# A hybrid encoder layer on one core: low parts of the mix weights moved to VectorE, the first norm's setup reordered, and the last down products written out in order

## The chip, the cores and the metric

The kernel runs on one core of a Trainium2 chip. The metric is the device time of one execution in microseconds (us). The core has TensorE for matrix products, VectorE, ScalarE and GpSimd for the rest, and a sequencer, SyncE (SP), which here only issues DMAs. The profile calls them PE (PEld for its weight loads), DVE, ACT, POOL and SP. TensorE's results go to PSUM, eight banks of 128 x 512 f32.

## The reference

One encoder layer over 512 tokens of width 1024, all in float32:

```
h = layer_norm(x, ln_in_g, ln_in_b)
mix = parallel_mixer(h, ...)      # window attention and dilated attention, each rms-normed,
                                  # side by side, times w_mix_out (1024 x 1024)
h = layer_norm(ALPHA * h + mix, ln1)
h = layer_norm(ALPHA * h + memory_cross_attention(h, mem_n), ln2)
ff = (gelu(conv3(h @ w_gate)) * (h @ w_up)) @ w_down     # inner width 2816
out = layer_norm(ALPHA * h + ff, ln3)
```

## The kernel before, in words

**Products.** Each float32 operand of a large product is split into a high part `hi` (a copy in a shorter format, ScalarE, line 136) and a low part `lo = raw - hi` (line 138), and a product is three matmuls: hi by hi, hi by lo, lo by hi (`mm`, line 168). Weights arrive in tiles `raw` of 128 x 1024 f32 (512 KB; three buffers) and become `hi` and `lo` (six buffers each). The low part is made on VectorE unless a caller names another engine; before the change `load_win` and `load_dil` name `nc.gpsimd` for the eight tiles of `w_mix_out`.

**Tokens** stand in four blocks `b` of 128. Accumulators are PSUM tiles: tags `t` and `o` with one bank each, `g` with two tiles of one bank, `s` with two tiles of two banks. A tile of two banks is one tile to the program that places waits: whoever writes one of its halves waits for those who read the other.

**Order.** Where the code stands in `manual_schedule(engines=...)`, the named engines run in the order of the text. Elsewhere a planner orders each engine's instructions by its own estimate of when they can run; `pin()` holds the next product at its place in the text. In the start (from line 371) TensorE, VectorE and ScalarE keep the order of the text; in the mix and behind it only TensorE does. The gate, up and down loops, from line 1350 on, are planned.

**Start.** `x` and the first weights of `w_in` are loaded on SP's queue. The first norm's scale and shift (`ln_in_g`, `ln_in_b`) are brought to all partitions by a product: `rows` (the tile `vt`) is zeroed, 128 x 1024 for each, one row of it is filled by a DMA, and a tile of ones (in `zs`) times it fills PSUM. The scale goes from there to `gin` by ScalarE (line 382), the shift stays in PSUM (an `s` tile, both halves). A float32 matmul of this kind is two instructions. `busy(n)` issues n products of the ones tile with itself, as work that nobody reads: `WARM[0]` of them ahead of the scale's product, `WARM[1]` behind the shift's. Then for block 0: `gain` (line 338: less the mean, times the scale), `shift` (line 345: times the root, plus the shift) on VectorE, and `turn` (line 352), transposes with `ident`, a part of the constants `cst`.

**Mix.** After attention the dilated outputs `oA` and `oB` are combined column tile by column tile (lines 1043 to 1051, `split_gain` at 924 and 925), while TensorE works at the memory's keys and values and then at the mix: for each half of the columns `load_win`, and for each block four k tiles of products into a `g` tile, which line 1119 adds to `h` on VectorE. Only then is the `g` tile free for the block after next. `load_dil` and the dilated part follow.

**Down.** 22 k tiles of `w_down`; the accumulators of all four blocks stand in PSUM together: block 0 in `t` and `o`, blocks 1 and 3 in one `s` tile each, block 2 in two `g` tiles. The first 16 k tiles go k by k over all blocks. For the last six the text goes block by block, half by half of the columns, and behind each half VectorE adds it to `h` (line 1408) and takes its statistics (1411). Behind both come `moments`, the norm (1415, 1416), and the output's DMA on SP (1417). Which block's products come when is the planner's.

Of the kernel before, what the change touches and what calls it, by code (L numbers as in the profile page):

```python
# [9 lines left out]
F32 = mybir.dt.float32  # L10
# [38 lines left out]
]  # L49

MEM_AT = (2, 0)
WARM = (6, 6)
CI, CF, CS, CMA, CM1, CM3 = 0, 128, 129, 130, 514, 770
CW = 898

# [16 lines left out]
def hymba_layer(ctx: ExitStack, tc: tile.TileContext, A, cst_d, out):  # L72
# [16 lines left out]
    cst = cpool.tile([P, CW], F32, name="cst")  # L89
    ident = cst[:, CI : CI + P]  # L90
    mhalf = cpool.tile([P, 1], F32, name="mhalf")
    nc.vector.memset(mhalf, -0.5)
    ones = cpool.tile([P, 2], F32, name="ones")
    nc.vector.memset(ones, 1.0)
    halfpi = cpool.tile([P, 1], F32, name="halfpi")
    nc.vector.memset(halfpi, HALF_PI)
    def halves(t):
        return [t[:, i * 512 : (i + 1) * 512] for i in range(2)]

# [41 lines left out]
    def wsplit(raw, shape, eng=None):  # L141
        return split(raw, shape, wpool, "hi", 6, wpool, "lo", 6, eng)
# [52 lines left out]
    def ps_tile(tag, bufs, shape=None):  # L195
        return gpool.tile(shape or [P, 512], F32, tag=tag, bufs=bufs, name=tag)
# [44 lines left out]

    zs = mkv.tile([P, 4, S], F32, tag="km", name="zs")
    ones_t = zs[:, 0, 0:P]
    nc.vector.memset(ones_t, 1.0)
    vt = mkv.tile([P, NB, 512], F32, tag="vm", name="vt")
    rows = vt.rearrange("p (v n) f -> p v n f", v=2)
    for v, name in enumerate(("ln_in_g", "ln_in_b")):
        nc.vector.memset(rows[:, v], 0.0)
        nc.scalar.dma_start(rows[0:1, v].rearrange("p n f -> p (n f)"), A[name].partition_broadcast(1))
    nc.scalar.dma_start(cst[:, 0:CMA], cst_d[:, 0:CMA])  # L250
    gin = wpool.tile([P, D], F32, tag="gb", bufs=2, name="gin")
    gt = halves(gin)
    sbt = s_tile()
# [115 lines left out]
        nc.scalar.dma_start(h_dram[b * P : (b + 1) * P, :], ah)  # L369

    with tc.manual_schedule(engines={nc.tensor.engine, nc.vector.engine, nc.scalar.engine}):
        spare = ps_tile("t", 1)

        def busy(n, ps=None):
# [556 lines left out]
    with tc.manual_schedule(engines={nc.tensor.engine}):  # L931
# [160 lines left out]
        def load_win(c0):  # L1092
            wa = w_mix[0:512, c0 : c0 + 512].rearrange("(s j d) f -> s d j f", s=2, d=HD)
            wts = []
            for i in range(2):
                raw = wpool.tile([P, 2, 512], F32, tag="raw", bufs=3, name="raw")
                for s2 in range(2):
                    nc.sync.dma_start(raw[s2 * HD : (s2 + 1) * HD], wa[s2][:, 2 * i : 2 * i + 2, :])
                wts.append(wsplit(raw, [P, 2, 512], nc.gpsimd))
            return wts  # L1100

        def load_dil(c0):
            return [w_rows(w_mix, 4 + 2 * i, 2, c0, 512, nc.gpsimd) for i in range(2)]

        def mix_part(ps, wts, b, k0, t):
            for k in range(4):
# [261 lines left out]
    with gs:  # L1368
        acc = [[ps_tile("t", 1), ps_tile("o", 1)]]
        for b in range(1, NB):  # L1370
            two = s_tile() if b != 2 else None
            acc.append([g_tile(), g_tile()] if two is None else [two[:, i, :] for i in range(2)])
        KO = NF - 6

        def down_q(k, w, a, b, f, a_):
            whi, wlo = w
            ahi, alo = a
            t = slice(b * P, (b + 1) * P)
            o = acc[b][f.start // 512][:, a_]
            mm(o, ahi[:, t], whi[:, 0, f], k == 0, False)  # L1380
            mm(o, ahi[:, t], wlo[:, 0, f], False, False)
            mm(o, alo[:, t], whi[:, 0, f], False, k == NF - 1)

        def down_k(k, w, a, b):
            for i in range(2):
                down_q(k, w, a, b, slice(i * 512, (i + 1) * 512), slice(0, 512))

        def down_ops(k):
            w = w_rows(A["w_down"][0], k, 1, 0, D)
            a = split(act[:, k, :], [P, S], xpool, "x", 12, xpool, "x", 12)  # L1390
            return w, a

        for k in range(KO):
            w, a = down_ops(k)
            for b in range(NB):
                down_k(k, w, a, b)
        last = [down_ops(k) for k in range(KO, NF)]
        o2 = out.rearrange("o s d -> (o s) d")
        for b in range(NB):
            q = 2  # L1400
            st = spool.tile([P, q, 6], F32, tag="stq", bufs=1, name="st")
            w_ = D // q
            for i in range(q):
                f = slice(i * w_, (i + 1) * w_)
                a_ = slice(i * w_ % 512, i * w_ % 512 + w_)
                for n, (w, a) in enumerate(last):
                    down_q(KO + n, w, a, b, f, a_)
                nc.vector.scalar_tensor_tensor(  # L1408
                    h[b][:, f], h[b][:, f], ALPHA, acc[b][i * w_ // 512][:, a_], ALU.mult, ALU.add
                )  # L1410
                nc.vector.bn_stats(st[:, i, :], h[b][:, f])
            mv, rs = moments(st)
            for i in range(2):
                f = slice(i * 512, (i + 1) * 512)
                nc.vector.scalar_tensor_tensor(h[b][:, f], h[b][:, f], mv[:, 0:1], g3[:, f], ALU.subtract, ALU.mult)
                nc.vector.scalar_tensor_tensor(h[b][:, f], h[b][:, f], rs, b3[:, f], ALU.mult, ALU.add)
                nc.sync.dma_start(o2[b * P : (b + 1) * P, f], h[b][:, f])


_INS = [  # L1420
# [25 lines left out]
```

## Time and profile before

| | us |
|---|---|
| three runs | 930.78, 929.01, 922.87 |
| their median | 929.01 |
| the profiled execution | 924.79 |
| its span, first to last instruction | 922.9 |
| mean granted TensorE clock | 0.995 |

The profile is of one execution. Rows of the time line give start, duration, engine, line, operation, out<-in, shapes and count of merged instructions; brackets give the idle time of the engine ahead of it and what ended it. A matmul is shown longer than its place in the pipeline: 128x512 is shown as 0.39 us, while the starts stand 0.227 us apart. Engine names ending in q are DMA issues.

### The profile page before, as it was taken

The numbers are of one execution on the slowest core, as the hardware profiler recorded it, in microseconds if no ns is written. First come the engines' busy times: TensorE is split into PE (matmuls) and PEld (weight loads), VectorE is DVE, ScalarE is ACT, GpSimd is POOL, SyncE is SP. The second block draws the span as 40 slices with busy tenths as digits, with TensorE's granted clock in tenths as the row PEclk, the third lists the DMA queues.
The fourth block names the chain that finished last, engine by engine and source line by source line (L and its number), as shares of the span: only waits on it lengthen the run. The fifth ranks groups of instructions, "written<-read, shape, count | busy, mean of one in ns | idle before, by whom it ended". The sixth has DMA issues, their size and how long they took to land.

```text
span 922.9 us, 12172 instructions
## 1 busy us (share of the span) xinstructions
PE 904.8 (98%) x4803; PEld 759.9 (82%) x4803; DVE 499.0 (54%) x853; ACT 361.9 (39%) x636; POOL 147.4 (16%) x109
## 2 busy tenths in 40 slices
PE   8999999999999999899999999999999999999996
PEld 6778987898878898688988889888888888888885
DVE  7965145435456666769466585554334434433346
ACT  4573436416455576215454223442233233222310
POOL 0054024332444426310000010000000000000001
PEclk9999999999999999999999999999999999999998
DMA  5762041314222337315222315433333332223201
GB/s 215 215 219 69 23 137 47 90 48 116 69 69 69 92 124 207 125 47 162 90 69 69 92 31 157 117 109 94 108 94 92 93 112 92 92 92 101 81 24 69
DMA packets 116939, 92.80 MB, mean 101 GB/s; under 512 B 12472, under 2 KB 100752, under 8 KB 116882
## 3 DMA queue, kind: packets, MB, share of 16 engines
q1 hardware_dynamic: 116048, 89.80, 32.1%
q10 hardware_dynamic: 834, 2.22, 0.6%
q8 instruction: 38, 0.62, 0.3%
q14 instruction: 19, 0.16, 0.1%
HBM read 87.82 MB, written 4.19 MB: 100 GB/s over the span
## 4 chain that ended last, share of the span: by engine, by line
PE 54%; DVE 2%; DMA 0%; issue 0%; ACT 0%; DVEq 0%; ACTq 0%
PE g L168 25%; PE s L168 21%; PE t L168 4%; PE o L168 4%; PE s L208 1%; DMA raw<-in_w_up_dram 0%; PE s L1220 0%; DVE lo L138 0%; DVE sd L1051 0%; DVE Ulo L214 0%; DVE mx L1201 0%; DVE h L126 0%; DVE h L124 0%; DVE h L1408 0%; ACT hi L136 0%
## 5 line engine op out<-in xcount | busy, mean ns | idle before, releaser
L138 DVE TENSOR_TENSOR lo<-raw,hi 128x1024 fp32r<-128x1024 f32 x134 | 167.2, 1248 | 153.5 <-ACT hi L136 151.2
L136 ACT CAST hi<-raw 128x1024 fp32r<-128x1024 f32 x142 | 149.2, 1052 | 225.4 <-PE g L168 151.0
L109 POOL TENSOR_TENSOR rs<-ve,mhalf 128x1 f32<-128x1 f32 x18 | 15.3, 852 | 534.6 <-DVE ve L115 526.3
L168 PE MATMUL g<-Thi,hi 128*128 128x512 f32 x240 | 94.9, 395 | 0.0
L168 PE MATMUL g<-Tlo,hi 128*128 128x512 f32 x240 | 94.4, 393 | 0.0
L168 PE MATMUL g<-Thi,lo 128*128 128x512 f32 x240 | 94.1, 392 | 0.0
L168 PE MATMUL g<-Uhi,hi 128*128 128x512 f32 (+1 forms) x256 | 93.3, 364 | 0.0
L168 PE MATMUL g<-Uhi,lo 128*128 128x512 f32 (+1 forms) x256 | 92.9, 363 | 0.0
L168 PE MATMUL g<-Ulo,hi 128*128 128x512 f32 (+1 forms) x256 | 92.9, 363 | 0.0
L525 POOL TENSOR_TENSOR zs<-zs,rsn 128x512 f32<-128x512 f32 x29 | 59.3, 2045 | 147.3 <-DVE zs L524 147.3
L168 PE MATMUL g<-hi,Thi 128*128 128x512 f32 x184 | 72.4, 403 | 3.5 <-DVE h L1119 3.5
L168 PE MATMUL g<-hi,Tlo 128*128 128x512 f32 x184 | 71.8, 400 | 0.5 <-DVE Tlo L1168 0.5
L168 PE MATMUL g<-lo,Thi 128*128 128x512 f32 x184 | 71.2, 398 | 0.4 <-DVE lo L279 0.4
L168 PE MATMUL s<-Uhi,lo 128*128 128x512 f32 x160 | 62.3, 390 | 0.0
L168 PE MATMUL s<-Ulo,hi 128*128 128x512 f32 x160 | 62.3, 390 | 0.0
L168 PE MATMUL s<-Uhi,hi 128*128 128x512 f32 x160 | 62.3, 389 | 0.0
L523 DVE TENSOR_TENSOR zs<-g,rc 128x512 f32<-128x512 f32 x29 | 20.0, 688 | 68.4 <-PE g L168 31.5
L168 PEld LDWEIGHTS g<-Uhi,lo 128*128 128x128 f32 x256 | 48.3, 189 | 7.5
L168 PEld LDWEIGHTS g<-Ulo,hi 128*128 128x128 f32 x256 | 48.3, 189 | 7.4
L168 PEld LDWEIGHTS g<-Uhi,hi 128*128 128x128 f32 x256 | 48.3, 189 | 7.4
L168 PEld LDWEIGHTS g<-Thi,hi 128*128 128x128 f32 x240 | 45.1, 188 | 11.0 <-issue 0.9
L168 PEld LDWEIGHTS g<-Tlo,hi 128*128 128x128 f32 x240 | 45.1, 188 | 10.3 <-issue 1.4
(330 smaller groups left out, 1796.5 us busy)
## 6 DMA issues: line engine op xcount, KB each, us to landing
raw<-in_w_in_dram SPq DMA_DIRECT2D x37, 512.0 KB, 3.8
raw<-in_w_gate_dram SPq DMA_DIRECT2D x22, 512.0 KB, 3.8
raw<-in_w_up_dram SPq DMA_DIRECT2D x22, 512.0 KB, 3.9
raw<-in_w_down_dram SPq DMA_DIRECT2D x22, 512.0 KB, 3.2
raw<-in_w_xk_dram SPq DMA_DIRECT2D x8, 512.0 KB, 3.9
raw<-in_w_xv_dram SPq DMA_DIRECT2D x8, 512.0 KB, 3.3
raw<-in_w_xq_dram SPq DMA_DIRECT2D x8, 512.0 KB, 4.7
raw<-in_w_xo_dram SPq DMA_DIRECT2D x8, 512.0 KB, 3.3
```

The lines of the kernel that those rows point to most:

```text
L109: nc.gpsimd.tensor_tensor(out_, in_, mhalf, ALU.pow)
L136: nc.scalar.copy(hi, raw)
L138: (eng or nc.vector).tensor_tensor(lo, raw, hi.bitcast(F32), ALU.subtract)
L168: on_pe(nc.tensor.matmul(o, l, r, start=first, stop=last))
L208: on_pe(nc.tensor.transpose(ps[:, i // 4, f : f + P], t[:, i * P : (i + 1) * P], ident))
L523: nc.vector.tensor_tensor(zc, ps, rc, ALU.mult)
L525: nc.gpsimd.tensor_tensor(sh, sh, rsn, ALU.mult)
```

## The change

`WARM` goes from (6, 6) to (12, 3). The ones tile, the zeros of the shift row and the three small constants go from VectorE to GpSimd; the zeros of the scale row stay on VectorE, which has no memset ahead of them any more. The three DMAs of ScalarE's queue (scale row, shift row, constants) go into the block in which ScalarE keeps the order of the text; before, they stood ahead of it and the constants were issued first. The low parts of the mix weights go from GpSimd to VectorE. The last six k tiles of the down products go into a block in which TensorE keeps the order of the text: blocks 1, 3, 0, 2, both halves of a block's products ahead of the additions and statistics of either.

```diff
--- before.py
+++ after.py
@@ -49,7 +49,7 @@
 ]
 
 MEM_AT = (2, 0)
-WARM = (6, 6)
+WARM = (12, 3)
 CI, CF, CS, CMA, CM1, CM3 = 0, 128, 129, 130, 514, 770
 CW = 898
 
@@ -89,11 +89,9 @@
     cst = cpool.tile([P, CW], F32, name="cst")
     ident = cst[:, CI : CI + P]
     mhalf = cpool.tile([P, 1], F32, name="mhalf")
-    nc.vector.memset(mhalf, -0.5)
     ones = cpool.tile([P, 2], F32, name="ones")
-    nc.vector.memset(ones, 1.0)
     halfpi = cpool.tile([P, 1], F32, name="halfpi")
-    nc.vector.memset(halfpi, HALF_PI)
+
     def halves(t):
         return [t[:, i * 512 : (i + 1) * 512] for i in range(2)]
 
@@ -241,13 +239,13 @@
 
     zs = mkv.tile([P, 4, S], F32, tag="km", name="zs")
     ones_t = zs[:, 0, 0:P]
-    nc.vector.memset(ones_t, 1.0)
+    nc.gpsimd.memset(ones_t, 1.0)
     vt = mkv.tile([P, NB, 512], F32, tag="vm", name="vt")
     rows = vt.rearrange("p (v n) f -> p v n f", v=2)
-    for v, name in enumerate(("ln_in_g", "ln_in_b")):
-        nc.vector.memset(rows[:, v], 0.0)
-        nc.scalar.dma_start(rows[0:1, v].rearrange("p n f -> p (n f)"), A[name].partition_broadcast(1))
-    nc.scalar.dma_start(cst[:, 0:CMA], cst_d[:, 0:CMA])
+    for v in range(2):
+        (nc.vector, nc.gpsimd)[v].memset(rows[:, v], 0.0)
+    for t, value in ((mhalf, -0.5), (ones, 1.0), (halfpi, HALF_PI)):
+        nc.gpsimd.memset(t, value)
     gin = wpool.tile([P, D], F32, tag="gb", bufs=2, name="gin")
     gt = halves(gin)
     sbt = s_tile()
@@ -369,6 +367,9 @@
         nc.scalar.dma_start(h_dram[b * P : (b + 1) * P, :], ah)
 
     with tc.manual_schedule(engines={nc.tensor.engine, nc.vector.engine, nc.scalar.engine}):
+        for v, name in enumerate(("ln_in_g", "ln_in_b")):
+            nc.scalar.dma_start(rows[0:1, v].rearrange("p n f -> p (n f)"), A[name].partition_broadcast(1))
+        nc.scalar.dma_start(cst[:, 0:CMA], cst_d[:, 0:CMA])
         spare = ps_tile("t", 1)
 
         def busy(n, ps=None):
@@ -1096,11 +1097,11 @@
                 raw = wpool.tile([P, 2, 512], F32, tag="raw", bufs=3, name="raw")
                 for s2 in range(2):
                     nc.sync.dma_start(raw[s2 * HD : (s2 + 1) * HD], wa[s2][:, 2 * i : 2 * i + 2, :])
-                wts.append(wsplit(raw, [P, 2, 512], nc.gpsimd))
+                wts.append(wsplit(raw, [P, 2, 512]))
             return wts
 
         def load_dil(c0):
-            return [w_rows(w_mix, 4 + 2 * i, 2, c0, 512, nc.gpsimd) for i in range(2)]
+            return [w_rows(w_mix, 4 + 2 * i, 2, c0, 512) for i in range(2)]
 
         def mix_part(ps, wts, b, k0, t):
             for k in range(4):
@@ -1396,25 +1397,22 @@
                 down_k(k, w, a, b)
         last = [down_ops(k) for k in range(KO, NF)]
         o2 = out.rearrange("o s d -> (o s) d")
-        for b in range(NB):
-            q = 2
-            st = spool.tile([P, q, 6], F32, tag="stq", bufs=1, name="st")
-            w_ = D // q
-            for i in range(q):
-                f = slice(i * w_, (i + 1) * w_)
-                a_ = slice(i * w_ % 512, i * w_ % 512 + w_)
-                for n, (w, a) in enumerate(last):
-                    down_q(KO + n, w, a, b, f, a_)
-                nc.vector.scalar_tensor_tensor(
-                    h[b][:, f], h[b][:, f], ALPHA, acc[b][i * w_ // 512][:, a_], ALU.mult, ALU.add
-                )
-                nc.vector.bn_stats(st[:, i, :], h[b][:, f])
-            mv, rs = moments(st)
-            for i in range(2):
-                f = slice(i * 512, (i + 1) * 512)
-                nc.vector.scalar_tensor_tensor(h[b][:, f], h[b][:, f], mv[:, 0:1], g3[:, f], ALU.subtract, ALU.mult)
-                nc.vector.scalar_tensor_tensor(h[b][:, f], h[b][:, f], rs, b3[:, f], ALU.mult, ALU.add)
-                nc.sync.dma_start(o2[b * P : (b + 1) * P, f], h[b][:, f])
+        pin()
+        with tc.manual_schedule(engines={nc.tensor.engine}):
+            for b in (1, 3, 0, 2):
+                st = spool.tile([P, 2, 6], F32, tag="stq", bufs=1, name="st")
+                fs = [slice(i * 512, (i + 1) * 512) for i in range(2)]
+                for f in fs:
+                    for n, (w, a) in enumerate(last):
+                        down_q(KO + n, w, a, b, f, slice(0, 512))
+                for i, f in enumerate(fs):
+                    nc.vector.scalar_tensor_tensor(h[b][:, f], h[b][:, f], ALPHA, acc[b][i], ALU.mult, ALU.add)
+                    nc.vector.bn_stats(st[:, i, :], h[b][:, f])
+                mv, rs = moments(st)
+                for f in fs:
+                    nc.vector.scalar_tensor_tensor(h[b][:, f], h[b][:, f], mv[:, 0:1], g3[:, f], ALU.subtract, ALU.mult)
+                    nc.vector.scalar_tensor_tensor(h[b][:, f], h[b][:, f], rs, b3[:, f], ALU.mult, ALU.add)
+                    nc.sync.dma_start(o2[b * P : (b + 1) * P, f], h[b][:, f])
 
 
 _INS = [
```

## Rows read from the trace of the kernel before

**Rows 1.** The page, busy time of the engines: us, share of the span, instructions.

```profile
PE 904.8 (98%) x4803; PEld 759.9 (82%) x4803; DVE 499.0 (54%) x853; ACT 361.9 (39%) x636; POOL 147.4 (16%) x109
```

**Rows 2.** The view by stretches: the stretch and its length, then busy us (instructions) of PE, PEld, DVE, ACT and POOL, the granted clock, the DMA engines' share, GB/s.

```profile
0.00:13.00 13.00, 9.29 (x32) 6.16 (x32) 6.41 (x14) 3.40 (x4) 0.75 (x5) 1.00 0.87 329
13.00:41.00 28.00, 27.07 (x137) 21.96 (x137) 26.34 (x45) 17.36 (x25) 1.63 (x3) 1.00 0.54 157
...
402.00:432.00 30.00, 30.00 (x146) 25.11 (x147) 27.75 (x45) 9.52 (x12) 3.98 (x4) 1.00 0.30 87
...
910.00:923.00 13.00, 4.59 (x19) 3.30 (x18) 8.60 (x16) 0.00 (x0) 1.83 (x2) 0.79 0.30 110
```

**Rows 3.** The time line of the first 14 us, all engines.

```profile
0.73 0.41 ACTq L250 DMA_DIRECT2D cst<-in_constants_dram  x1
...
0.80 0.06 DVE L92 MEMSET mhalf<- 128x1 f32 x1 [0.80 <-PEq L1431]
...
1.14 2.93 PE L168 MATMUL t<-zs 128*128 128x128 f32 x12 [1.14 <-DVE zs L244]
...
1.25 0.91 DVE L248 MEMSET vt<- 128x1024 f32 x1 [0.16 <-issue]
...
2.19 0.49 ACTq L249 DMA_DIRECT2D vt<-in_ln_in_g_dram  x1
...
6.64 3.38 PE L168 MATMUL g<-vt,zs 128*128 128x512 f32 x4 [2.58 <-DMA vt<-in_ln_in_g_dram]
...
9.86 1.88 PE L168 MATMUL s<-vt,zs 128*128 128x512 f32 x4
...
11.58 1.50 PE L168 MATMUL t<-zs 128*128 128x128 f32 x12
...
11.84 1.41 DVE L345 SCALAR_TENSOR_TENSOR oA<-oA,rs,s 128x512 f32<-128x512 f32 x2 [0.41 <-PE s L168]
...
13.14 0.65 PE L352 MATMUL t<-cst,oA 128*128 128x128 f32 x4
```

**Rows 4.** The time line of GpSimd near 343 us: a memset of 512 columns.

```profile
343.33 0.52 POOL L1001 MEMSET stw<- 128x512 f32 x1
```

**Rows 5.** Groups of instructions by form, 340 to 405 us: the low parts on GpSimd and on VectorE. Busy us, mean ns of one, idle time ahead of them.

```profile
L138 POOL TENSOR_TENSOR lo<-raw,hi 128x1024 fp32r<-128x1024 f32 x8 | 21.2, 2666 | 18.0 <-ACT hi L136 17.9
...
L138 DVE TENSOR_TENSOR lo<-raw,hi 128x1024 fp32r<-128x1024 f32 x5 | 6.1, 1220 | 4.1 <-ACT hi L136 4.1
```

**Rows 6.** The time line in the mix: GpSimd, then VectorE.

```profile
356.20 16.06 POOL L138 TENSOR_TENSOR lo<-raw,hi 128x1024 fp32r<-128x1024 f32 x6 [5.88 <-ACT hi L136]
...
361.54 0.69 DVE L1043 TENSOR_TENSOR oA<-oA,s 128x512 f32<-128x512 f32 x1 [1.86 <-PE s L168]
...
362.86 1.97 DVE L1045 TENSOR_TENSOR oA<-oA,oB 128x512 f32<-128x512 f32 x1
...
367.04 2.98 DVE L925 SCALAR_TENSOR_TENSOR Tlo<-oA,gdc,Thi 128x512 fp32r<-128x512 f32 x1 [1.02 <-ACT Thi L924]
369.94 2.87 DVE L1045 TENSOR_TENSOR oA<-oA,oB 128x512 f32<-128x512 f32 x1
373.60 0.75 DVE L925 SCALAR_TENSOR_TENSOR Tlo<-oA,gdc,Thi 128x512 fp32r<-128x512 f32 x1 [0.79 <-ACT Thi L924]
...
375.47 0.74 DVE L1119 SCALAR_TENSOR_TENSOR h<-g,raw__3058,h 128x512 f32<-128x512 f32 x1
...
377.33 0.69 DVE L1045 TENSOR_TENSOR oA<-oA,oB 128x512 f32<-128x512 f32 x1
...
379.79 0.74 DVE L925 SCALAR_TENSOR_TENSOR Tlo<-oA,gdc,Thi 128x512 fp32r<-128x512 f32 x1
...
387.20 2.88 DVE L1051 TENSOR_TENSOR sd<-sd,oB 128x512 f32<-128x512 f32 x1
390.00 1.40 DVE L1119 SCALAR_TENSOR_TENSOR h<-g,raw__3058,h 128x512 f32<-128x512 f32 x2
```

**Rows 7.** The time line of TensorE about its two waits in the mix.

```profile
373.28 0.39 PE L168 MATMUL g<-hi,Tlo 128*128 128x512 f32 x1
376.27 0.50 PE L168 MATMUL g<-hi,Thi 128*128 128x512 f32 x1 [2.60 <-DVE h L1119]
...
389.52 0.39 PE L168 MATMUL g<-hi,Tlo 128*128 128x512 f32 x1
390.80 0.50 PE L168 MATMUL g<-hi,Thi 128*128 128x512 f32 x1 [0.89 <-DVE h L1119]
```

**Rows 8.** The view by stretches, columns as in rows 2: the stretch from 378.4 us.

```profile
378.40:381.50 3.10, 3.10 (x8) 2.45 (x8) 2.73 (x5) 0.89 (x2) 0.00 (x0) 0.50 0.45 169
```

**Rows 9.** The last down products: a row of the chain of waits (start, us, what) where they begin; the time line of VectorE at the last k tile and at the end, and of TensorE at the end.

```profile
881.66 3.40 PE t L168 x15
...
883.08 1.23 DVE L138 TENSOR_TENSOR lo<-raw,hi 128x1024 fp32r<-128x1024 f32 x1 [0.26 <-ACT hi L136]
...
915.41 0.69 DVE L1408 SCALAR_TENSOR_TENSOR h<-h,s 128x512 f32<-128x512 f32 x1 [0.91 <-PE s L168]
...
909.83 0.39 PE L168 MATMUL s<-hi,lo 128*128 128x512 f32 x1
911.00 0.50 PE L168 MATMUL s<-hi 128*128 128x512 f32 x1 [0.78 <-DVE h L1408]
...
914.99 0.39 PE L168 MATMUL s<-hi,lo 128*128 128x512 f32 x1
```

## The prediction

> **What bounds the kernel now.** First the page's table of engines: TensorE is busy for 904.8 of the 922.9 us span, VectorE for 499.0 [rows 1]. So an edit pays only where it removes idle or slow TensorE time, 18 us of idle in all. The view by stretches says where that lies [rows 2]: 3.71 us in the first 13 us (9.29 busy), 0.93 us from 13 to 41 and none from 402 to 432, although VectorE works 26.34 of 28 and 27.75 of 30 us there, and 8.41 us in the last 13 us. The time line then names the wait at each place: the first norm's scale row [rows 3], `h`, line 1119, twice in the mix [rows 7], and `h`, line 1408, once in the last down products [rows 9]. The three edits of the change lie at these three places, so their savings add. Between them TensorE's order is written out or pinned and it works without rest, so an earlier arrival at 13 us, at 402 us and at 881 us is kept.
>
> **Start.** Now VectorE makes three small memsets and the ones tile, and zeroes the scale row from 1.25 to 2.16. The row's DMA is issued at 2.19, the product that waits for it starts at 6.64, 4.45 us later, after TensorE has rested for 2.58 us [rows 3]. With the row's memset first on VectorE (from 0.80, the start of its first one) and 0.91 us long, the issue comes at 1.74, 0.45 us sooner. With the same 4.45 us the products can start at 6.19.
>
> Whether the 24 warm-up instructions (two for each of 12 calls) are done by then, and at which clock the rest runs, decides the size. The granted clock reads 1.00 from 0 to 13 us [rows 2], but the durations show two levels a factor of two apart, 1.2 and 2.4 GHz: twelve warm-up instructions take 2.93 us at the start and 1.50 us from 11.58; the four of the scale row take 3.22 us from start to start (6.64 to 9.86), the four of the shift row 1.72 (9.86 to 11.58) [rows 3]. Before the pace rose, TensorE had worked from 6.64 on; in the first stretch, 1.14 to 4.07, it rested before it could rise. The change replaces this rest by work. All 24 at the low level take 24 x 0.244 = 5.9 us and end at 7.0; with seven or more of them at the high one they end by 6.2. I take the high level from 6.2 on: scale row 6.2 to 7.9, shift row to 9.64, against 11.58: 1.94 us sooner. Of the closing warm-up 6 instructions go instead of 12 (0.75 us), to about 10.4, so it is not late. VectorE's shift waits for both halves of the shift row, now 0.26 us (11.84 against 11.58), then works 1.41 us: its end moves from 13.25 to 11.31, and with it the transposes of 13.14. **Start: 1.9 us.** Bounds: all warm-up and scale products at the low level, 7.0 + 3.22 + 1.72 = 11.94, a loss of 0.4; a row that lands 0.5 us sooner still, because the constants' DMA no longer stands ahead of it on ScalarE's queue, a gain of 2.4.
>
> What is moved costs nothing by these covers. The ones tile, the shift row's zeros and three small constants go to GpSimd: 512 columns take 0.52 us there [rows 4], so 1024 take about 1.0 and the shift row's DMA can go at about 2.3, right behind the scale row's, where it went at 3.27; its product is wanted at 7.9. TensorE's first product waits for the ones tile on GpSimd, now the first thing there. The constants' DMA, 65 KB, drops from 0.73 to about 2.5, third on ScalarE's queue ahead of its first copy, and is wanted by the transposes at 11; with DMA engines full from 3 to 14 us it may take 6 us and still land by 9. No queue of SP is changed.
>
> No row shows a memset of VectorE beside one of GpSimd. The nearest are two-input operations of both, where VectorE's takes up to 2.2 us more [rows 6]. If the memset suffered the whole length of GpSimd's, 1.0 us, the issue would be at 2.7 and the start's gain some 1.0 us. I keep 1.74, since neither memset reads anything. The Trainium skill ("SBUF — State Buffer", Who interferes with whom) says that a VectorE instruction with at most one SBUF input, outside its two-port modes, doesn't contend with GpSimd; by it the sum stays at 1.9, by the stretched rows it would be 1.0. No run here shows it yet.
>
> **Mix weights.** GpSimd makes eight low parts at 2.666 us each; VectorE makes the same tile in 1.220 [rows 5]. So VectorE gets 8 x 1.22 = 9.8 us more. But while GpSimd works, VectorE's own operations stretch: `oA`, line 1045, takes 1.97 and 2.87 us against 0.69, `Tlo`, line 925, 2.98 against 0.74, and `sd`, line 1051, of the same shape as `oA`, 2.88 [rows 6]. That is 1.28 + 2.24 + 2.18 + 2.19 = 7.9 us on these four alone, and all four stand ahead of an addition (line 1119) that TensorE waits for.
>
> First stall: from 361.54 to 375.47 VectorE's row of operations leads to the addition of block 0, which gives back the accumulator that TensorE wants at 373.5 (0.23 after its product of 373.28); it gets it at 376.27 [rows 6, 7]. Lost: 2.99 - 0.23 = 2.76 us. Behind the stall the granted clock falls to 0.50, the 1.2 GHz level, for 378.4 to 381.5 [rows 8]: half of 3.1 us, 1.55 us, is lost too. After the change this stretch loses 5.7 us of stretching and gains about three of the low parts, 3.7 us (GpSimd begins six at 356.20, so the first three have their place before 361.5). The addition then starts 2.0 us sooner, at 373.5, and TensorE goes on 0.8 us later as now, at 374.3: 0.8 us of stall are left if nothing else moves. Of the present 13.9 us VectorE also spends 1.8 waiting, 1.02 of it ahead of 367.04 for ScalarE's `Thi`, which itself follows a stretched line 1045; without that no stall is left. A stall of 0.8 us ended at full clock at 390.80 [rows 7], so I count the slow stretch as gone either way. Second stall: 389.52 to 390.80, less 0.23, 1.05 us, where `sd` at 2.88 stands ahead of the addition of 390.00 [rows 6, 7]. After it two low parts on VectorE (2.4 us) replace the stretch, but VectorE has been free for some 3 us before, since the first stall is gone. Sum 2.76 + 1.55 + 1.05 = 5.4; with a rest of 0.4 us, **5.0 us**. Bounds: 5.4, and for the other end the third rival. What is next late is VectorE itself in 402 to 432, 27.75 busy of 30 [rows 2], which the change leaves alone. GpSimd has nothing else to do here.
>
> **Last down products.** 144 products lie in 881.7 to 915.4. They follow each other 0.227 us apart but for one place: block 3's second half stands in the shared two-bank tile whose first half VectorE must first read (line 1408); 909.83 to 911.00 [rows 9], 0.94 us too long, and a first step of about 0.1 more. In the written order both halves of a block are multiplied before either is read, and the blocks in shared tiles (1, 3) come first. So the wait has no place, and block 2, last, has a tile for each half: its first half is read during the second, as now. The tail from the last product, 914.99, to VectorE's read at 915.41 and the span's end stays as it is. Price of the order: six rows of k stand in the first half of block 1, the last one wanted 15 products after 881.66, at 885.06. Its low part begins at 883.08, behind the high one, and is done at 884.31 [rows 9]; 0.75 us of room. If planning delays them by 1 us, 0.25 us is lost. **1.0 us**, bounds 0 and 1.05.
>
> **Sum.** 1.9 + 5.0 + 1.0 = 7.9 us. The profiled execution took 924.79 us, 922.9 of span and 1.9 around it; by it the new time is 916.9. The three shown runs are 922.87 to 930.78 with the median at 929.01, so the profiled one is a low draw. The middle of the four times, 926.9, less 7.9 gives **919.0**.
>
> **Rivals.** (1) The mix pays nothing: the low parts stand ahead of the additions on VectorE's queue, waiting for ScalarE's high parts and their DMAs, and the additions come as late as now. For it: VectorE works in order, and the plan, not the kernel's text, places the parts. Against: the count above. 926.9 - 2.9 = 924.0. (2) The start pays nothing: warm-up at the low level to its end, with the row waiting behind it: 0.4 lost, 6.0 won elsewhere, 921.3. For it: the first 12 instructions never left the low level. (3) Slower than before: VectorE's long operations are not stretched by GpSimd. Then the five low parts behind 361.5 come on top, 6.1 us of TensorE waiting, and the slow clock lasts as long again, 1.55; less 2.9, 4.8 us slower, 931.7. It decides if line 925, 1045 or 1051 still shows over 1.8 us after the change while the low parts stand on VectorE. Against it: the same lines take 0.69 and 0.74 when GpSimd rests [rows 6].
>
> **How the numbers follow.** Chances: forecast 0.65, rival 1 0.16, rival 2 0.14, rival 3 0.05. The shown runs spread 4 us either way, which the range must carry: low end 926.9 - 8.9 (all upper bounds) less 4 to 6 is 912; high end, rival 1 with 3 us, is 927. 1% is 9.3 us, about what a measurement of this kernel can tell from no change. The forecast is at 0.85%, so with the spread and upper bounds some half of it lies beyond 1%; with small parts of rivals 1 and 2: 0.38 faster, 0.58 within, 0.04 slower.
>
> **What would show it.** Right: ScalarE's queue issues the scale row at about 1.75; its product starts near 6.2 at 0.43 us a step; transposes near 11.2; lines 925, 1045, 1051 all under 0.8 us in the mix, no wait of TensorE for line 1119 above 0.8 us and no stretch of granted clock 0.50; 144 last products in 32.6 us. Wrong: warm-up at 0.24 us to its end, TensorE idle in the mix, or a new wait at the first k rows of the last block.

## The result, and the profile after

| | before | after |
|---|---|---|
| executions, us | 922.87 to 930.78, six of them | 915.96 to 916.83, six of them |
| median | 926.51 | 916.34 |
| profiled execution / its span | 924.79 / 922.9 | 916.33 / 914.6 |

The ratio is 0.9891, with a 95% interval of 0.986 to 0.9923: 1.1% faster. By the medians it is 10.2 us, by the two profiled executions 8.3 us of span. The difference between these two numbers is a finding of its own (experiments e11 and e12). The spread shrinks as well, from 8 us to 0.9 us.

Three marks in the trace divide the 8.3 us. The first is the transposes of the second block, `t<-cst,oB`, with which the start's influence on the order ends. The second is the first product `s<-rh,sel` to the first product `o<-ones,sd`, here called the mix stage. The third is the start of the last six k tiles to the last addition of line 1408 (1409 after).

| | before | after | difference |
|---|---|---|---|
| transposes of the second block | 25.95 | 24.71 | -1.2 |
| mix stage, 360.78 to 401.82 and 359.36 to 394.73 | 41.04 | 35.37 | -5.7 |
| last products, 881.66 to 915.41 and 874.37 to 907.05 | 33.75 | 32.68 | -1.1 |

The sum is 8.0 of 8.3; the stretches between the marks (24.71 to 359.36, 394.73 to 874.37) give the other 0.4, and rounding takes the rest.

The page's row of busy engines, answering to [rows 1]:

```profile
PE 903.1 (99%) x4809; PEld 760.0 (83%) x4809; DVE 497.2 (54%) x856; ACT 362.3 (40%) x636; POOL 127.5 (14%) x106
```

GpSimd loses 19.9 us of work, and VectorE, which took over eight tiles of 1.22 us and gave away some small memsets, is not busier than before (499.0): its own operations have become shorter by about as much. The view by stretches, columns as in [rows 2]:

```profile
0.00:13.00 13.00, 11.28 (x50) 8.81 (x51) 6.45 (x11) 4.22 (x6) 1.95 (x10) 1.00 0.88 331
...
300.00:386.00 86.00, 85.67 (x560) 73.00 (x559) 63.45 (x109) 51.30 (x96) 14.95 (x10) 1.00 0.48 147
...
402.00:432.00 30.00, 30.00 (x171) 26.20 (x170) 29.55 (x47) 12.55 (x16) 3.88 (x4) 1.00 0.46 130
```

In the first 13 us TensorE is busy 11.28 us instead of 9.29. From 300 to 386 us it rests 0.33 us, at a granted clock of 1.00. From 402 us VectorE is busier than before (29.55 of 30 us), and TensorE still does not rest.

The time line of the start, answering to [rows 3]:

```profile
0.87 0.96 POOL L246 MEMSET vt<- 128x1024 f32 x1
0.99 5.39 PE L166 MATMUL t<-zs 128*128 128x128 f32 x24 [0.99 <-POOL zs L242]
1.02 0.91 DVE L246 MEMSET vt<- 128x1024 f32 x1 [1.02 <-PEq L1429]
1.96 0.52 ACTq L371 DMA_DIRECT2D vt<-in_ln_in_g_dram  x1
...
6.84 1.95 PE L166 MATMUL g<-vt,zs 128*128 128x512 f32 x4 [0.45 <-DMA vt<-in_ln_in_g_dram]
...
8.63 1.88 PE L166 MATMUL s<-vt,zs 128*128 128x512 f32 x4
...
10.61 1.40 DVE L343 SCALAR_TENSOR_TENSOR oA<-oA,rs,s 128x512 f32<-128x512 f32 x2 [0.41 <-PE s L166]
...
11.46 0.63 PE L350 MATMUL t<-cst,oA 128*128 128x128 f32 x4 [0.28 <-PE t L166]
```

The scale row's product starts 0.20 us later than before (6.84 against 6.64). What is shorter is the product itself, 1.79 us from start to start against 3.22. VectorE's shift (line 343), which leads to the transposes, ends at 12.01 instead of 13.25; that is the 1.2 us of the first mark.

Groups by form in the mix, 340 to 405 us, answering to [rows 5, 6], and TensorE's waits in the whole execution, the longest first (us in total, times, longest):

```profile
L136 DVE TENSOR_TENSOR lo<-raw,hi 128x1024 fp32r<-128x1024 f32 x13 | 15.8, 1222 | 6.4 <-ACT hi L134 6.3
...
L926 DVE SCALAR_TENSOR_TENSOR Tlo<-oA,gdc,Thi 128x512 fp32r<-128x512 f32 x4 | 3.0, 743 | 0.0
...
L1046 DVE TENSOR_TENSOR oA<-oA,oB 128x512 f32<-128x512 f32 x4 | 2.7, 681 | 0.0
```

```profile
PE t L166 <- POOL zs L242: 1.0, 1, 1.0
PE g L166 <- DVE Tlo L1169: 0.5, 1, 0.5
PE g L166 <- DMA vt<-in_ln_in_g_dram: 0.5, 1, 0.5
PE g L166 <- DVE lo L277: 0.4, 1, 0.4
```

No operation of VectorE is stretched in the mix any more, and neither the addition to `h` in the mix (line 1120, 1119 before) nor that of the last products (line 1409) is among the waits.

The end, answering to [rows 9]: the chain of waits (start, us, what), and then the last addition on VectorE's time line.

```profile
873.01 17.68 PE s L166 x78
890.69 4.08 PE t L166 x18
894.77 4.08 PE o L166 x18
898.85 8.17 PE g L166 x36
```

```profile
907.05 0.69 DVE L1409 SCALAR_TENSOR_TENSOR h<-h,g 128x512 f32<-128x512 f32 x1 [2.33 <-PE g L166]
```

These are blocks 1 and 3 (`s`, of which the first 6 instructions belong to the k tile before), 0 (`t`, `o`) and 2 (`g`): each piece begins where the one before ends, 0.227 us an instruction. From the last addition to the span's end it is 7.5 us in both kernels.

### The profile page after: what moved, and what is told of

Its sections match the earlier page's. It is cut to its first block, busy times and chain, and to the rows that moved or that the text cites. A ratio compares the mean times of both kernels' runs of the same rounds, so it can differ in the third digit from the quotient of the medians.

```text
span 914.6 us, 12181 instructions
## 1 busy us (share of the span) xinstructions
PE 903.1 (99%) x4809; PEld 760.0 (83%) x4809; DVE 497.2 (54%) x856; ACT 362.3 (40%) x636; POOL 127.5 (14%) x106
## 4 chain that ended last, share of the span: by engine, by line
PE 95%; DVE 3%; DMA 1%; issue 0%; ACT 0%; POOL 0%; DVEq 0%; ACTq 0%
PE g L166 53%; PE s L166 27%; PE t L166 4%; PE o L166 4%; PE o L690 3%; PE s L678 2%; PE s L206 1%; DMA vt<-in_ln_in_g_dram 1%; PE s L1221 0%; DVE lo L277 0%; DVE oA L343 0%; DVE st L307 0%; DVE Tlo L362 0%; POOL zs L526 0%; DVE mx L1202 0%
## 5 line engine op out<-in xcount | busy, mean ns | idle before, releaser
L136 DVE TENSOR_TENSOR lo<-raw,hi 128x1024 fp32r<-128x1024 f32 x142 | 176.7, 1246 | 156.9 <-ACT hi L134 154.6
L134 ACT CAST hi<-raw 128x1024 fp32r<-128x1024 f32 x142 | 149.2, 1052 | 221.1 <-PE g L166 163.3
```

The lines of the kernel that those rows point to most:

```text
L134: nc.scalar.copy(hi, raw)
L136: (eng or nc.vector).tensor_tensor(lo, raw, hi.bitcast(F32), ALU.subtract)
```

## The experiments

The kernel before ran beside them on the same chips, with medians of 926.85 us (e1 to e4), 925.08 (e5 to e8) and 925.05 (e9, e10). Each ratio is to the runs beside it.

**e1: the low parts alone.** The kernel before, with one edit:

```diff
-                wts.append(wsplit(raw, [P, 2, 512], nc.gpsimd))
+                wts.append(wsplit(raw, [P, 2, 512]))
...
-            return [w_rows(w_mix, 4 + 2 * i, 2, c0, 512, nc.gpsimd) for i in range(2)]
+            return [w_rows(w_mix, 4 + 2 * i, 2, c0, 512) for i in range(2)]
```

> The kernel before with one part of the change: the eight low parts of the mix weights on VectorE. Theory: TensorE's two waits for line 1119 and the slow-clock stretch behind them go (5.4 us worked out, 5.7 read off the two traces between 367 and 403 us), start and last products stay as before: about 920.8 against a median before of 926.5, 917.2 of span. Rival: part of the mix's gain needs the earlier start, and this one gives 3 us or less (923.5 or more). On the spread of the runs of before (922.9 to 930.8): if it comes from how VectorE's and GpSimd's operations meet in the mix, the runs of this kernel lie within 1.5 us of each other; if it comes from the start, they spread as before.

Measured: 920.21 us (919.98 to 921.89), ratio 0.9932 (0.9908 to 0.9956), 6.6 us less than the 926.85 beside it. The mix stage runs from 362.01 to 397.38, 35.37 us, as in after. The wait for line 1408 is still there with 0.8 us, the wait for the row with 2.7. So the mix edit alone brings all that the mix stage gains. It also takes most of the spread away: these four executions lie 1.9 us apart (at most 1.5 were expected), the thirteen of the kernel before beside them 8.2.

**e2: the change without it.** After, with these two lines as they were before.

> The changed kernel with the eight low parts back on GpSimd. Theory: both waits and the slow-clock stretch return, 916.3 + 5.7 = 922.0, and the runs spread over several us again. Rival: with the start 1.4 us earlier the parts meet otherwise and less than 3 us come back (919 or less).

Measured: 919.63 us (918.94 to 922.84), ratio 0.9929 (0.99 to 0.9957). The edit is worth 3.3 us here and 6.6 us in e1; 5.7 had been expected here, less than 3 by the rival. In the profile of e2 TensorE waits for line 1120 twice, the longest wait is 1.7 us, and the clock behind it stays up (view by stretches, columns as in [rows 2]):

```profile
PE g L166 <- DVE h L1120: 2.6, 2, 1.7
```

```profile
373.00:381.00 8.00, 7.22 (x30) 5.46 (x31) 7.45 (x13) 2.80 (x4) 0.73 (x1) 1.00 0.31 119
```

Its mix stage takes 38.59 us, 2.45 less than the first profile of before. That is the first wait, 2.60 - 1.69 = 0.91, and the slow stretch, 1.55. The slow stretch, which was expected back, is not there. The same low parts on GpSimd, then, cost differently much from one execution to the next; e11 and e12 show that for the kernel before. Whether the earlier start also makes the cheap case more frequent, four executions can't tell.

**e3 and e4: is it GpSimd's reading that stretches VectorE?** After, with GpSimd work beside the low parts whose result nobody reads. In e3 it reads the tile, in e4 it writes, and reads only two elements per partition (the second diff stands in place of the `tensor_tensor` of the first):

```diff
+        def beside(pair):
+            hi, junk = pair[0].bitcast(F32), oW[:, 0:2, :]
+            nc.gpsimd.tensor_tensor(junk, hi, hi, ALU.subtract)
+            return pair
...
-                wts.append(wsplit(raw, [P, 2, 512]))
+                wts.append(beside(wsplit(raw, [P, 2, 512])))
...
-            return [w_rows(w_mix, 4 + 2 * i, 2, c0, 512) for i in range(2)]
+            return [beside(w_rows(w_mix, 4 + 2 * i, 2, c0, 512)) for i in range(2)]
```

```diff
+            nc.gpsimd.tensor_tensor(junk[:, 0, 0:1], hi[:, 0, 0:1], hi[:, 1, 0:1], ALU.subtract)
+            for _ in range(3):
+                nc.gpsimd.memset(junk, 0.0)
```

> The changed kernel, low parts on VectorE, and beside each of the eight one GpSimd subtraction of the high part from itself (128x1024, two SBUF inputs, 2.7 us) whose result nobody reads; VectorE's order is the same as in the changed kernel. Theory (GpSimd's reads stretch VectorE): lines 926, 1046 and 1052 show 1.8 to 2.9 us again, line 1120's addition (here line 1125) comes late, TensorE waits and its clock falls; with eight low parts more on VectorE than before at least the 5.7 us come back, 922 to 928. Rival (what the change gave is that the low parts and their buffers are ready earlier): nothing changes, 916 to 917.

> As the last one, but GpSimd's work beside each low part is three memsets of 128x1024 (some 2.9 us, it only writes) behind a one-column subtraction that ties them to the high part; VectorE's order is again that of the changed kernel. The Trainium skill (SBUF - State Buffer, Who interferes with whom) says that an instruction of VectorE with two SBUF inputs contends with a GpSimd instruction that reads SBUF, not with one that only writes it: by it 916 to 917, lines 926, 1046 and 1052 at 0.68 to 0.75. Rival: any work of GpSimd stretches VectorE, 922 to 928 as with the reads.

Measured: e3 926.3 us (923.87 to 927.26), ratio 1.0003 (0.9982 to 1.0023); e4 916.94 us (916.75 to 917.16), ratio 0.9893 (0.9866 to 0.992). VectorE runs the same operations in the same order in e3 and in after. Groups by form, 340 to 410 us, of e3 and then of e4:

```profile
L1095 POOL TENSOR_TENSOR oW<-hi 128x1024 f32<-128x1024 f32 x8 | 21.6, 2701 | 22.7 <-ACT hi L134 22.3
...
L136 DVE TENSOR_TENSOR lo<-raw,hi 128x1024 fp32r<-128x1024 f32 x13 | 22.2, 1712 | 6.9 <-ACT hi L134 6.9
...
L926 DVE SCALAR_TENSOR_TENSOR Tlo<-oA,gdc,Thi 128x512 fp32r<-128x512 f32 x4 | 4.6, 1151 | 0.0
```

```profile
L1097 POOL MEMSET oW<- 128x1024 f32 x24 | 22.9, 956 | 1.4
...
L136 DVE TENSOR_TENSOR lo<-raw,hi 128x1024 fp32r<-128x1024 f32 x13 | 15.9, 1222 | 7.5 <-ACT hi L134 7.4
...
L926 DVE SCALAR_TENSOR_TENSOR Tlo<-oA,gdc,Thi 128x512 fp32r<-128x512 f32 x4 | 3.0, 747 | 0.0
```

GpSimd is busy about as long in both (21.6 us reading, 22.9 writing). Only the reading stretches VectorE: the mean low part takes 1712 ns against 1222, and the mix stage 46.81 us against 35.36. In e3 TensorE waits three times in it, for 2.89, 2.96 and 2.04 us. The stretching falls on the low parts above all, up to 2.9 us each; lines 926 and 1046 show 2.38 us once each and line 1052 stays at 0.68, so the 1.8 to 2.9 us expected on those three came only in part. That is the prediction's mechanism, shown alone, and the low parts are as open to it as the other operations. The Trainium skill ("SBUF — State Buffer", Who interferes with whom) says that a VectorE instruction with two SBUF inputs contends with a GpSimd instruction that reads SBUF, not with one that only writes it. These two runs agree, and so does line 1043, which takes one of its inputs from PSUM: 0.69 us in [rows 6], beside the same GpSimd operations that stretch line 1045.

**e5: the warm-up as before, the rest of the change kept.**

```diff
-WARM = (12, 3)
+WARM = (6, 6)
```

> The changed kernel with WARM back at (6, 6): TensorE rests again between its twelfth warm-up instruction (3.9 us) and the scale row. Theory (the start's gain is the clock, not the row): the row lands as in the changed kernel, between 5.9 and 6.9 us, the four scale instructions take 2.6 to 3.2 us instead of 1.8, the transposes come near 12.6 to 13, and the time is 917.4 to 918.0 against 916.3. Rival (the gain is the earlier issue of the row): 916.3 to 916.6.

Measured: 918.94 us (918.35 to 921.02), ratio 0.9943 (0.9922 to 0.9963), 2.6 us more than after and 0.9 above the expected 917.4 to 918.0. The time line:

```profile
5.82 3.75 PE L166 MATMUL g<-vt,zs 128*128 128x512 f32 x4 [1.90 <-DVE ve L113]
...
9.36 2.17 PE L166 MATMUL s<-vt,zs 128*128 128x512 f32 x4
...
12.93 0.66 PE L350 MATMUL t<-cst,oA 128*128 128x128 f32 x4
```

The product starts a full microsecond earlier than in after, and the transposes still come 1.5 us later: it takes 3.54 us from start to start, at the 1.2 GHz level, after TensorE had rested for 1.90 us. (The row names line 113 as the end of that rest; the product reads nothing of it, and by the program it waits for the scale row.)

**e6: the warm-up of after, the memsets and DMAs as before.**

```diff
+    nc.vector.memset(mhalf, -0.5)
...
+    nc.vector.memset(ones, 1.0)
...
+    nc.vector.memset(halfpi, HALF_PI)
...
-    nc.gpsimd.memset(ones_t, 1.0)
+    nc.vector.memset(ones_t, 1.0)
...
-    for v in range(2):
-        (nc.vector, nc.gpsimd)[v].memset(rows[:, v], 0.0)
-    for t, value in ((mhalf, -0.5), (ones, 1.0), (halfpi, HALF_PI)):
-        nc.gpsimd.memset(t, value)
+    for v, name in enumerate(("ln_in_g", "ln_in_b")):
+        nc.vector.memset(rows[:, v], 0.0)
+        nc.scalar.dma_start(rows[0:1, v].rearrange("p n f -> p (n f)"), A[name].partition_broadcast(1))
+    nc.scalar.dma_start(cst[:, 0:CMA], cst_d[:, 0:CMA])
...
-        for v, name in enumerate(("ln_in_g", "ln_in_b")):
-            nc.scalar.dma_start(rows[0:1, v].rearrange("p n f -> p (n f)"), A[name].partition_broadcast(1))
-        nc.scalar.dma_start(cst[:, 0:CMA], cst_d[:, 0:CMA])
```

> The changed kernel with WARM (12, 3), but memsets on VectorE, DMAs and their order as before (constants first at 0.73, scale row issued at 2.19). Theory (the row's landing is set by full DMA engines, not by its issue 0.23 us earlier): the products start between 6.2 and 7.0 as in the changed kernel, 916.2 to 916.8. Rival (the prediction's step: issue earlier, landing earlier by as much): 0.2 to 0.5 us more than the changed kernel, with the product not before 7.0.

Measured: 916.31 us (916.02 to 916.45), ratio 0.9911 (0.9892 to 0.993): the time of after. The row is issued at 2.19 instead of 1.96, its product starts at 6.99 instead of 6.84, the transposes at 11.61 instead of 11.46. So the moved zeros and DMAs are worth nothing that the medians show; as far as they tell, the longer warm-up is the start's whole gain.

**e7, e9, e10: the row without zeros.** If the product takes one partition, nothing has to be zeroed and the row's DMA can go at once. e7 does this for both rows, e9 for the scale row only, e10 is e9 with `WARM = (10, 3)`.

```diff
...
-            mm(gps[n], ones_t, rows[:, 0, n, :], True, True)
+            mm(gps[n], ones_t[0:1, :], rows[0:1, 0, n, :], True, True)
...
```

> The changed kernel with the scale and shift products over one partition instead of 128: no zeroing at all (rows and their other 127 partitions are not read), so the scale row's DMA is issued at about 0.75, ahead of most of the large transfers. The result is the same. Theory (the landing depends on what stands in the DMA engines ahead of it): it lands by 5, the products follow the warm-up without a wait (5.6 to 6.4 us), 915.5 to 916.2. Rival (a small transfer takes its 4.4 to 4.8 us whatever the load, and the wait was 0.5 us): the same 915.8, landing at 5.2 to 5.5; the landing time tells them apart. If TensorE at one partition does not reach its higher clock, the products take 0.81 us each and the time is 917 or more.

> The changed kernel with only the scale row's two products over one partition (no zeros for it, its DMA issued at about 0.75); the shift row keeps its zeros, now on VectorE, and its products over 128 partitions. The result is the same. Theory (in the run without any zeros the clock fell behind 3.6 us of one-partition products, and the row itself was in time): half as many of them leave the clock up, the products follow the warm-up at 5.9 without a wait, the shift's end moves from 12.0 to about 11.1, 915.3 to 915.8. Rival (any one-partition products let the clock fall): granted clock 0.50 again between 8 and 15 us, 916.5 to 917.5.

> As the last one with WARM (10, 3): four warm-up instructions fewer, so the scale row's products can start at about 5.2. Theory: if the clock is up by then, 0.4 us earlier again, 915.0 to 915.5; if it isn't (in the runs so far the pace rose between 4.5 and 6.1 us), the scale products run at half pace and nothing is won, 915.5 to 916.5, with a wider spread.

Measured: e7 916.86 us (915.61 to 917.5), e9 916.22 (915.49 to 916.75), e10 915.23 (914.56 to 918.94), ratios 0.9916 (0.9894 to 0.9937), 0.9902 (0.9878 to 0.9927) and 0.9898 (0.9874 to 0.9923). In all three the row is issued at 0.73 and is not waited for; the warm-up is what ends last. In e7 the clock fell although TensorE did not rest, and the 915.5 to 916.2 expected with the clock up were missed (view by stretches):

```profile
8.00:9.00 1.00, 1.00 (x3) 0.41 (x2) 0.89 (x2) 1.00 (x2) 0.00 (x0) 0.83 1.04 399
9.00:15.00 6.00, 5.94 (x23) 4.35 (x21) 4.30 (x9) 2.01 (x4) 0.55 (x1) 0.50 0.94 324
```

In e9, with the shift row's product on all partitions, it stayed up, the product started at 6.00 and the transposes at 10.84. The mean granted clocks of all executions agree: 0.995 or 0.996 in the six of e7, 0.997 or 0.998 in the six of e9. Yet e9 is 0.4 us above the 915.3 to 915.8 that were expected, the time of after within its spread. In e10 the product and the transposes start at 5.15 and 9.99, the latter 1.5 us ahead of after. One of the six executions of e10 took 918.94, 2.8 us above the next; no trace shows why. e10 is 1.1 us ahead of after by medians, as expected, and the intervals of the two overlap.

**e8: the last products with each half read as soon as it is done.** After, with the addition back between the halves:

```diff
-                for f in fs:
+                for i, f in enumerate(fs):
                     for n, (w, a) in enumerate(last):
                         down_q(KO + n, w, a, b, f, slice(0, 512))
-                for i, f in enumerate(fs):
                     nc.vector.scalar_tensor_tensor(h[b][:, f], h[b][:, f], ALPHA, acc[b][i], ALU.mult, ALU.add)
```

> The changed kernel with the last down products in the same written order of blocks, but VectorE's addition and statistics of a half placed between the two halves' products, as the text of the kernel before had them. Theory (the wait for line 1408 came from two halves in one shared tile): TensorE waits about 0.8 us, 1.05 in all, at the second half of block 1 and of block 3, none at blocks 0 and 2: 916.3 + 2.1 = 918.4. Rival (the wait came from the planner's order alone): no wait, 916.3.

Measured: 918.76 us (917.87 to 919.03), ratio 0.9936 (0.9917 to 0.9955), 2.4 us more than after (2.1 were expected). The waits of TensorE:

```profile
PE s L166 <- DVE h L1408: 1.9, 2, 1.1
```

They are at 879.43 and 888.99, in blocks 1 and 3, whose halves share a tile, and not in blocks 0 and 2, whose halves have a tile each. The shared tile makes the wait, not the closeness of the addition.

**e11, e12: the kernel before again, twice, for two more profiles.**

> The kernel before once more, unchanged, for a second profile: its executions lie 921 to 931 us apart, and their mean granted clocks 0.991 to 0.999. Theory (the spread is the clock, which falls behind the stall for line 1119 in the mix): stages before 360 us as in the first profile within 1 us; a wait for line 1119 of 2 to 3 us, and behind it a stretch at 0.50 whose length times one half, with the stall, carries the difference of span: span 921 with no such stretch, 923 with 3 us of it, 926 with 8 to 10 us of it. Rival (the spread is in the start or elsewhere): the mix stage takes 41.0 us again whatever the span, and other stretches of a clock below 1.00, or the landing of the first row, carry it.

> The same kernel a third time, for a third profile. Theory: from the first product of line 1043's operands to the first of the next stage 38.5 us without a stretch at 0.50, 41.0 with 3 us of it, 43 or more with 7 us of it, and the span follows by the same amount. Rival: the stage stays within 0.5 us of 41.0 in all three while the spans differ by more.

Measured: 926.97 us (span 925.1) and 921.32 us (span 919.5). First stall and clock in the mix of e11, then of e12 (each a fence of the time line and one of the view by stretches):

```profile
356.88 16.07 POOL L138 TENSOR_TENSOR lo<-raw,hi 128x1024 fp32r<-128x1024 f32 x6 [6.81 <-ACT hi L136]
...
367.76 2.94 DVE L925 SCALAR_TENSOR_TENSOR Tlo<-oA,gdc,Thi 128x512 fp32r<-128x512 f32 x1 [1.05 <-ACT Thi L924]
...
376.95 0.50 PE L168 MATMUL g<-hi,Thi 128*128 128x512 f32 x1 [3.55 <-DVE h L1119]
```

```profile
378.30:384.70 6.40, 6.40 (x15) 4.63 (x15) 4.97 (x8) 1.24 (x2) 0.00 (x0) 0.50 0.25 82
```

```profile
355.86 16.53 POOL L138 TENSOR_TENSOR lo<-raw,hi 128x1024 fp32r<-128x1024 f32 x6 [5.71 <-ACT hi L136]
...
366.51 0.80 DVE L925 SCALAR_TENSOR_TENSOR Tlo<-oA,gdc,Thi 128x512 fp32r<-128x512 f32 x1 [0.75 <-ACT Thi L924]
...
374.85 0.50 PE L168 MATMUL g<-hi,Thi 128*128 128x512 f32 x1 [1.38 <-DVE h L1119]
```

```profile
378.30:384.70 6.40, 6.40 (x30) 5.29 (x29) 4.83 (x8) 3.25 (x4) 3.35 (x2) 1.00 0.21 68
```

| | e12 | first profile | e11 |
|---|---|---|---|
| GpSimd begins its six low parts | 355.86 | 356.20 | 356.88 |
| first `Tlo`, line 925 | 0.80 | 2.98 | 2.94 |
| first `oA`, line 1045 | 1.83 | 1.97 | 2.92 |
| lines 1045 and 925 twice each, ahead of the addition | 7.55 | 8.57 | 9.49 |
| first wait of TensorE for line 1119 | 1.38 | 2.60 | 3.55 |
| clock 0.50 behind it | none | 3.1 us | 6.4 us |
| mix stage | 38.27 | 41.04 | 43.50 |
| span | 919.5 | 922.9 | 925.1 |

Transposes of the first block (13.14 to 13.21) and the first mix product (360.51 to 360.78) agree within 0.3 us in the three, so the mix stage carries the spread: 5.2 of 5.6 us of span. What differs is how long VectorE's operations are stretched: the stall grows from 1.4 to 3.6 us, and the slow stretch behind it from nothing to 6.4 us, of which half is lost. The theory's numbers hold within 0.5 us for the stage (38.5 and 43 or more were expected), the rival's 41.0 do not. The stall of 2 to 3 us that the theory of e11 expected in every execution missed: it is 1.38 and 3.55.

What chooses between the cheap and the dear case is not shown. GpSimd starts up to 1.0 us apart in the three, but the start alone does not order the profiles. Ahead of the first mix product it begins 4.72 us in e12, 4.58 in the first profile, 3.63 in e11, and 4.48 in e2, whose stall of 1.69 us lies below the 2.60 of the first profile. In e12 and e2, where the first `Tlo` takes 0.80 and 0.75 us, it is GpSimd that runs longer: 16.53 and 16.60 us for its six low parts, 16.06 and 16.07 in the other two.

In 35 executions of the kernel before that stood beside the experiments, the nine with a mean granted clock of 0.998 or 0.999 have a median of 922.9 us, the 21 with 0.995 or less one of 927.2. The five between lie at 921.4 to 923.8. For these 35 no trace shows where the clock fell.

## Why the prediction was right, and where not

It forecast 919.0 us, in a range of 912 to 927, and its likeliest case came; 916.34 is 2.7 us below. Its terms add up to 7.9 us where the two profiles differ by 8.3; the miss comes from the time that they were taken off, 926.9, for which they were too small, as the paragraph on the mix shows.

**What bounds the kernel**: right. The three places were independent: 1.2, 5.7 and 1.1 us stand in the marks, and e1, e5 and e8 each move one of them.

**Start, 1.9 us: size fair, two steps wrong.** The first is "the issue comes at 1.74, 0.45 us sooner. With the same 4.45 us the products can start at 6.19." VectorE's first memset began at 1.02, not 0.80, so the issue came at 1.96. And the 4.45 us are no fixed price: in the six profiles with the row issued at 1.96, its product started at 5.82 (e5), 5.89 (e3), 6.33 (e2), 6.84 (after), 6.87 (e4) and 7.29 (e8), that is 3.9 to 5.3 us behind the issue; in the five with an issue at 2.19 it started at 6.62 to 6.99. By medians, e6 shows that the earlier issue is worth nothing.

The second is "All 24 at the low level take 24 x 0.244 = 5.9 us and end at 7.0". The 0.244 is the shown length of a group, which includes the longer first step and the end of the last instruction. From start to start they stand 0.21 us apart, so in after all 24 ran at the low pace and still ended at 6.38; what the products then waited for was the row. That work in place of the rest brings the higher pace was right and carried the gain: both rows ran at 2.4 GHz (0.50 us for the first step, 0.43 for the others).

The product came 0.65 us later than forecast, and so the mark moved by 1.2 us instead of 1.9. This too is one draw. In the five profiles with this start (after, e2, e3, e4, e8) the mark lies 17.9 us behind the product's start, at 23.77 to 25.16, against 25.95 to 26.02 in the three profiles of before: a gain of 0.8 to 2.2 us. By medians e5 puts the longer warm-up at 2.6 us. Its profile shows 1.0 of it at the mark, 25.74 against 24.71, although its row came a microsecond sooner than in after; with the product at 6.38, where the warm-up of after ends, the same 17.9 us would put the mark at about 24.3, an estimate, and so the gain at some 1.5. Another 0.5 us are longer waits of TensorE for line 770 behind it.

**The memset beside GpSimd's**: right, 0.91 us beside 0.96 us of GpSimd's, as alone in [rows 3]. The other end, the whole length of GpSimd's memset, did not occur. e4 shows that memsets leave the two-input operations alone too.

**Mix, 5.0 us, bound 5.4: mechanism right, size low.** The trace of the same execution gives 5.67. "0.8 us of stall are left if nothing else moves" failed on its low side: none is left, and with it the rest of 0.4 us that I took off. TensorE issues the same 150 instructions in the same order in this stage before and after, so the 0.3 us above the bound can be placed: behind each of the two waits the next step takes 0.34 us instead of 0.23, which makes 0.2, and the last 0.1 is spread in small pieces. (The stall at 390.80 that the prediction calls 0.8 us stands as 0.89 in [rows 7]; nothing hangs on it.) What I did not see, and what makes the total come out 2.7 us high, is how far the size depends on the execution. [Rows 6 to 8] are one draw of three: 38.27, 41.04 and 43.50 against 35.37 make the edit worth 2.9, 5.7 and 8.1 us. I took the sum from the middle time, 926.9, and sized it on a profile that lay 2 us below; from that profile's own time the forecast was 916.9. e11, at 926.97, has the mix at 8.1 us, 3.1 more than forecast, and the start at 1.3 by its mark (25.97), 0.6 less: together 2.5 of the 2.7 us by which the forecast was high. That the mix of the sized profile was the middle one of three was luck: e12 would have offered it 2.9 us, e11 8.1.

**Last products, 1.0 us**: right, 1.07, and the reason is shown by e8. The six k rows of the new first block are not waited for.

**Rivals.** (1) fell: e1 gains 6.6 us by the mix edit alone. (2) fell: e5 costs 2.6 us. (3) fell: e3 and e4. Its own test, lines 925, 1045 and 1051 under 1.8 us, came out at 0.68 to 0.75.

## What to carry to other kernels

Where a profile shows an operation at several durations, ask what the neighbouring engine read at that time: work given back to a half-idle engine can cost less than the stretching that it takes away. Where a kernel's executions lie per cent apart, take more than one profile before sizing an edit: a single one gives the price of a stall in one draw (2.9, 5.7 or 8.1 us for the mix here, 0.8 to 2.2 us for the start). Filling the wait ahead of a first product with work that nobody reads can be worth more than making the wait shorter, as e5 and e6 show.

## What the runs showed of the hardware that was not expected

- A stall of 1.4 or 1.7 us in the mix (e12, e2) left the clock at 1.00; one of 2.60 was followed by 3.1 us at 0.50, one of 3.55 by 6.4 us. The length of the stall alone does not decide: in e3 the clock stayed at 1.00 behind a stall of 2.89 us (364.7 to 374.0), and was 0.50 behind the next, of 2.96 us (377.4 to 383.0):

```profile
364.74 0.73 PE L166 MATMUL s<-rh,sel 64*128 64x512 f32 x2 [2.89 <-DVE oB L1045]
...
377.45 0.80 PE L166 MATMUL g<-hi,Thi 128*128 128x512 f32 x1 [2.96 <-DVE h L1125]
```

- In e7 the granted clock fell during the last of eight products with one partition on the contracted side, four for the scale and four for the shift, and was 0.50 from about 9 to 15 us with TensorE 5.94 of 6.00 us busy. In e9, with four of them followed by four over all partitions, it was 1.00 from 8 to 15 us.
- When the row of 4 KB landed could not be told from its issue: its product started between 5.82 and 7.29 after an issue at 1.96 (six profiles), and between 6.62 and 6.99 after one at 2.19 (five). The DMA engines were 0.87 and 0.88 busy over the first 13 us.
- A GpSimd memset of 128x1024 f32 takes 0.96 us, next to VectorE's 0.91; a two-input operation of that shape 2.70 us (e3), against VectorE's 1.22.
